# First expert layer in unsplit float32, with the split parts' buffers lent to weights and to gathered rows

## The chip, the cores and the metric

The kernel is one program on one core of one Trainium2 chip. The metric is device time in microseconds, from the program's start to its end; less is better. A profiled execution lists every instruction of the engines: TensorE (PE for matmuls, PEld for weight loads), VectorE (DVE), ScalarE (ACT), GpSimd (POOL), and SyncE (SP), which here only issues DMAs.

## The reference

Two blocks run one after the other, in float32, on 256 tokens of width 1024. The first (gated state-space, linear recurrence and retention branches, then a convolutional FFN) makes x. The second has two layers over x and a context xc of 256 tokens; each layer mixes tokens and then adds an expert layer (`peer_ffn`), in layer 0 to both streams, in layer 1 to x alone. The change concerns the expert layer of layer 0, for x.

```python
def peer_ffn(h, wq, sub_keys, eu, ev):            # eu, ev: 16384 experts x 1024
    def one(t):                                   # t: 128 tokens x 1024
        q = (t @ wq).reshape(TOKEN_BLOCK, PEER_HEADS, 2, PEER_DK // 2)
        s = jnp.einsum("thpd,hpnd->thpn", q, sub_keys)
        st, it = lax.top_k(s, PEER_TOPK)          # 16 of 128 keys, twice a head
        ...                                       # best 16 of the 256 pairs
        e = jnp.take_along_axis(cidx, pos, axis=-1)
        g = jax.nn.softmax(best, axis=-1)
        u = jnp.take(eu, e, axis=0)               # 8 heads x 16 = 128 experts a token
        act = jax.nn.gelu(jnp.einsum("thkd,td->thk", u, t), approximate=False)
        return jnp.einsum("thk,thkd->td", (g * act), jnp.take(ev, e, axis=0))
...
    h2 = rmsnorm_2(x, norm2_g) * (1.0 + sc2) + sh2
    x = x + g2 * peer_ffn(h2, peer_wq, peer_keys, peer_u, peer_v)
    if need_ctx:                                  # layer 0
        ...
        xc = xc + g2c * peer_ffn(h2c, peer_wq, peer_keys, peer_u, peer_v)
```

## The kernel before

Activations lie with 128 of the 1024 channels on the partitions, as tiles of [128, 8, 256 tokens]. A weight tile is [128, 1024] float32 (8 blocks of 128 x 128). Two ways of multiplying exist. In the split way (`mm3`, L295) a weight is loaded to a buffer `raw`, ScalarE rounds it to a high part `whi` of type float32r (L257), VectorE or GpSimd subtracts to a low part `wlo` (L258), and TensorE makes 24 matmuls: high x high and high x low alternating (L301, L302), then low x high (L304). In the whole way (`W(..., True)`) the raw weight is multiplied by float32 activations in 8 matmuls, each of which the profile shows as two instructions.

`Stream` (L260) is the weight stream. The instance `W` has a ring of three `raw` buffers, and rings of three `whi` and three `wlo`, 4 KB a partition each; every load is issued by SyncE (L271). `pattern` says which engine makes the low parts: in the expert layer of layer 0 it is GpSimd ("G").

The expert layer has two forms. For the context of layer 0 it is sparse (`Sparse`, L1496): `work` makes 512 steps, and each gathers one expert row a token for 128 tokens by an indirect DMA that GpSimd issues (L1529), into one of four `gr` buffers, three rows ahead of use. In the first 256 steps VectorE multiplies the row with the tokens and sums it into a dot product (L1540); in the others it adds the row, times its weight, to `gy` (L1546, L1548). The steps are laid beside other work: `steps(n)` moves `work` on by n rows, and the program text has 86 of them in the token mixer of x in layer 0 before the dense layer begins.

For x the form is dense (`peer`, L1583): all 16384 experts are computed for all 256 tokens, and a matrix A of gate weights, mostly zero, picks those that count. `norm_split` (L364) makes the normed input, in layer 0 as high part `Hh`, low part `Hl` and whole `H`. `queries` (L1487) makes the keys' queries, `choose2` the top 16s, and `spread` (L1446) scatters them into A in DRAM. Then:

- `first` (L1614) is one unit: the weight `pu` for 128 experts, matmuls with the input into a bank `pp`, and a GELU on ScalarE to `gt` (L1623). In layer 0 odd units are whole (L1619), even ones split (L1621). 13 groups of 8 units, 104, are made ahead (L1650 to L1665) while choosing and spreading go on, and each `gt` is stored to DRAM (`GX`, L1657).
- `ustage` (L1673) loads A for a group of 8 units (`At`, L1678) and each `gt` again (L1684), or makes it for the last three groups, and multiplies the two (L1688). `vstage` (L1697) multiplies by `pv`, eight weight tiles `d` a group, whole in layer 0 (L1703), and adds to x (L1704).

`tick(0)` after each unit made ahead is `steps(1.0)`, `tick(1)` after each `d` is `steps(2.6)`, and `tick(2)` runs what is left and adds the context's result (`far.end`). `kept` is how many of the 104 tiles stay in SBUF in place of `GX`; it is 0 in layer 0 and 51 in layer 1.

The order of instructions on each engine is laid down when the kernel is built, by a scheduler that takes the program text as priority and its own estimate of when things are ready; on the chip each engine keeps that order. An engine can so be ahead of the text with work that was ready early.

Of the kernel before, what the change touches and what calls it, by code (L numbers as in the profile page):

```python
# [18 lines left out]
P = 128  # L19
T = 256  # L20
# [167 lines left out]
def build(tc, I, out, off, dbg=None):  # L188
# [71 lines left out]
    class Stream:  # L260
# [6 lines left out]
            s.turn, s.pattern = 0, pattern  # L267

        def __call__(s, ap, whole=False):
            raw = s.raw.tile([P, 1024], F32, name="raw")  # L270
            nc.sync.dma_start(raw, ap)  # L271
            if whole:
                return raw.rearrange("p (k n) -> p k n", k=8)
            hi = s.hl.tile([P, 1024], F32R, name="whi")
            lo = s.hl.tile([P, 1024], F32R, name="wlo")
            e = G if s.pattern[s.turn % len(s.pattern)] == "G" else V
            s.turn += 1
            split(hi, lo, raw, e)
            return hi.rearrange("p (k n) -> p k n", k=8), lo.rearrange("p (k n) -> p k n", k=8)
# [15 lines left out]
    def mm3(ps, w, x, ks=range(8), x0=0, start=True, stop=True):  # L295

        wh, wl = w
        xh, xl = x
        ks = list(ks)
        for j, k in enumerate(ks):  # L300
            PE.matmul(ps, wh[:, k], xh[:, x0 + k], start=start and j == 0, stop=False)  # L301
            PE.matmul(ps, wh[:, k], xl[:, x0 + k], start=False, stop=False)  # L302
        for j, k in enumerate(ks):
            PE.matmul(ps, wl[:, k], xh[:, x0 + k], start=False, stop=stop and j == len(ks) - 1)  # L304
# [59 lines left out]
    def norm_split(rg, x, rstd, gcol, shcol, hi, lo, whole=None):  # L364

        for k in range(8):
            h = rg.t1()
            V.scalar_tensor_tensor(h, x[:, k], gcol(k), rstd, op0=ALU.mult, op1=ALU.mult)
            if whole is not None:
                A.activation(whole[:, k], h, AF.Identity, bias=shcol(k))  # L370
            if shcol is None:
                A.activation(hi[:, k], h, AF.Copy)
                V.tensor_sub(lo[:, k], h, hi[:, k].bitcast(F32))
            else:
                A.activation(hi[:, k], h, AF.Identity, bias=shcol(k))
                V.scalar_tensor_tensor(lo[:, k], h, shcol(k), hi[:, k].bitcast(F32),  # L376
                                       op0=ALU.add, op1=ALU.subtract)
# [1106 lines left out]
                    nc.sync.dma_start(Ad[t * 8 + tg], stg.rearrange("p g e n k -> p (g e n k)"))  # L1484
                yield

    def queries(l, w, bk, sp, h):  # L1487
        n = h[0].shape[-1]
        q = sp.tile([P, 8, n], F32, name="pq", bufs=1)
        for hd in range(8):  # L1490
            ps = bk.proj()[:, :n]
            mm3(ps, w(I["wq"][l, hd]), h)
            A.activation(q[:, hd], ps, AF.Copy)
        return q

    class Sparse:  # L1496
# [1 line left out]


        def __init__(m, l, s, pool):  # L1500
            m.l, m.s = l, s
            tile_ = lambda shape, dt, name: pool.tile(shape, dt, name=name, bufs=1)
            m.h = tile_([P, 2, 1024], F32, "gh")
            m.idx = tile_([P, 2, P], U32, "gi")
            m.wt = tile_([P, 2, P], F32, "gw")
            m.dot = tile_([P, 2, P], F32, "gd")
# [12 lines left out]
        def work(m, pool, nbuf):  # L1519

            m.y = pool.tile([P, 2, 1024], F32, name="gy", bufs=1)
            todo = [(w, t, k) for w in range(2) for t in range(2) for k in range(P)]
            got = []

            def gather():
                if len(got) < len(todo):
                    w, t, k = todo[len(got)]
                    r = pool.tile([P, 1024], F32, name="gr", bufs=nbuf)
                    G.indirect_dma_start(r, None, I[("us", "vs")[w]],  # L1529
                                         bass.IndirectOffsetOnAxis(ap=m.idx[:, t, k:k + 1], axis=0))  # L1530
                    got.append(r)

            for _ in range(nbuf - 1):
                gather()
            for n, (w, t, k) in enumerate(todo):
                gather()
                r = got[n]
                got[n] = None
                if w == 0:
                    V.scalar_tensor_tensor(r, r, 1.0, m.h[:, t], op0=ALU.mult, op1=ALU.mult,  # L1540
                                           accum_out=m.dot[:, t, k:k + 1])
                    if k == P - 1:
                        A.activation(m.dot[:, t], m.dot[:, t], AF.Gelu)
                        V.tensor_mul(m.wt[:, t], m.wt[:, t], m.dot[:, t])
                elif k == 0:
                    V.tensor_scalar(m.y[:, t], r, m.wt[:, t, k:k + 1], None, op0=ALU.mult)  # L1546
                else:
                    V.scalar_tensor_tensor(m.y[:, t], r, m.wt[:, t, k:k + 1], m.y[:, t], op0=ALU.mult, op1=ALU.add)  # L1548
                yield
# [33 lines left out]
    def peer(l, streams, ahead, nproj, kept=0, side_work=None, tick=lambda n: None, ends=None):  # L1583
# [5 lines left out]
        s, = streams  # L1589
        xs = ExitStack()  # L1590
        hp = xs.enter_context(TP(f"H{l}"))
        Hh = hp.tile([P, 8, N], F32R, name="Hh")
        Hl = hp.tile([P, 8, N], F32R, name="Hl")
        gp = xs.enter_context(TP(f"pg{l}", 4))
        Ads = [dram.tile([16, P, 2048], F32, name=f"A{l}{s}") for s in streams]
        H = hp.tile([P, 8, N], F32, name="H") if l == 0 else None
        GX = dram.tile([ahead * 8 - kept, P, N], F32, name=f"GX{l}")
        gk = xs.enter_context(TP(f"pk{l}", kept, side="right")) if kept else None
        mark(f"norm2{l}")
# [3 lines left out]
        with TP(f"n2{l}") as sm:  # L1603
            rg = Ring(sm, 8, 0)
            for j in range(ns):
                norm_split(rg, X[s], rstd_cm(rg, bk.misc, X[s], 8, D), sc_col(l, 1, s), sh_col(l, 1, s),
                           Hh[:, :, j * T:(j + 1) * T], Hl[:, :, j * T:(j + 1) * T], H)
        Y, At, GT = {}, {}, {}

        na = ahead * 8  # L1610
# [2 lines left out]

        def first(g, j, pool=gp):  # L1614
            ps = bk.proj()[:, :N]
            if H is not None and j % 2:
                w = W(I["pu"][l, g * 8 + j], True)
                for k in range(8):
                    PE.matmul(ps, w[:, k], H[:, k], start=k == 0, stop=k == 7)  # L1619
            else:  # L1620
                mm3(ps, W(I["pu"][l, g * 8 + j]), (Hh, Hl))  # L1621
            gt = pool.tile([P, N], F32, name="gt")
            A.activation(gt, ps, AF.Gelu)  # L1623
            return gt

        with ExitStack() as ls:
            sp, sm, so = [ls.enter_context(TP(f"{n}{l}", 2)) for n in ("rt", "rs", "rz")]
            j = 0
            W.pattern = "G"
            q = queries(l, W, bk, sp, [z[:, :, j * T:(j + 1) * T] for z in (Hh, Hl)])  # L1630
            sls = [sp.tile([P, 2, P, 2, 2], F16, name="sl") for t in range(2)]
            bo = Banks(ls, f"po{l}", 0, 2)

            def pieces():
                mark(f"choose{l}{s}")
                for _ in choose2(l, q, sls, sm, bks.proj, bk):
                    yield 0.85
                    mark(f"choose{l}{s}")
                for t in range(2):
                    mark(f"spread{l}{s}")  # L1640
                    for _ in spread(sls[t], Ads[j], t, so, bo.misc):
                        yield 1.42
                        mark(f"spread{l}{s}")

            if side_work:
                side_work(ls)

            run, credit = pieces(), 0.0
            W.pattern = "G" if l == 0 else "GV"
            for g in range(ahead):  # L1650
                for i in range(8):
                    mark(f"ahead{l}")
                    n = g * 8 + i
                    if n in stay:
                        GT[n] = first(g, i, gk)
                    else:
                        nc.sync.dma_start(GX[place[n]], first(g, i))  # L1657
                    tick(0)
                    credit += 1
                    while credit > 0 and run:  # L1660
                        w = next(run, None)
                        if w is None:
                            run = None
                            break
                        credit -= 1 / w  # L1665
            for _ in run or ():
                pass
# [103 lines left out]
    if stages >= 2:  # L1771
        with ExitStack() as fr:
# [25 lines left out]
            if stages >= 3:  # L1798
                ends = []

                def tick(n):
                    if n < 2:
                        steps((1.0, 2.6)[n])
                    else:
                        for _ in run:
                            pass
                        far.end(ends[0])

                peer(0, (0,), 13, 3, 0, side, tick, ends)
        gs.close()  # L1810
    if stages >= 4:
        with ExitStack() as fs:
# [54 lines left out]
```

## Time and profile before

| | |
|---|---|
| median of 3 runs | 3745.09 us (3743.55 to 3750.69) |
| profiled execution: time, span | 3736.46 us, 3734.7 us |
| busy share of the span: PE, DVE, POOL, ACT | 84%, 68%, 44%, 35% |
| mean granted clock of TensorE | 0.927 |
| read from HBM, written | 823.34 MB, 55.18 MB |

The span is the time from the first instruction to the last; the little around it is the difference to the execution's time. An engine's busy share is an average over stages with different limits, so it doesn't name the limit of any one stage. A row of a lines view gives, after the count, the busy time, the mean duration in ns, then the idle time of the engine just before such instructions and what ended it.

### The profile page before, as it was taken

The page shows a single profiled execution, that of the slowest core. Times are in us where ns is not written, and L with a number is a line of the kernel's source. Part 1 is how long each engine was busy: PE and PEld are TensorE (multiplying, and loading weights), DVE is VectorE, ACT ScalarE, POOL GpSimd, SP SyncE. Part 2 cuts the span into 40 slices and gives each one's busy share as a digit, 9 for nine tenths or more (in the row PEclk, how much of TensorE's full clock was granted, in tenths as well). Part 3 has the DMA queues.
Part 4 walks back from the last instruction along what each step waited for, and adds up shares of the span by engine and source line. Part 5 has one row for each costly group of instructions (what it writes and reads, how often), then busy time and mean ns, then how long its engine had stood idle before and what let it go on. Part 6 is the DMA issues. An engine that isn't in the chain of part 4 may idle for free. (4 is left out here: it accounts for less than half of the span.)

```text
span 3734.7 us, 57168 instructions
## 1 busy us (share of the span) xinstructions
PE 3153.2 (84%) x21589; PEld 2856.7 (76%) x21589; DVE 2547.0 (68%) x4819; ACT 1298.9 (35%) x2302; POOL 1646.6 (44%) x1141
## 2 busy tenths in 40 slices
PE   8899987899675587777767877999888999999998
PEld 6699976899563376666656666888776999999998
DVE  7845757578988778978866666422655788677755
ACT  4544446454244122222200000011463546544443
POOL 1233213155677677777744444121663544322222
PEclk9999998999797799989888888999999999999999
DMA  7665541355785889899999999754434667877754
GB/s 246 245 185 160 162 130 51 116 181 178 232 290 163 309 282 306 306 341 352 357 382 355 382 364 365 267 169 163 130 119 162 197 195 272 278 237 244 242 198 136
DMA packets 327397, 882.29 MB, mean 236 GB/s; under 512 B 29521, under 2 KB 142161, under 8 KB 316753
## 3 DMA queue, kind: packets, MB, share of 16 engines
q1 hardware_dynamic: 252528, 607.65, 49.1%
q0 software_dynamic: 73872, 269.52, 19.9%
q8 instruction: 170, 2.79, 0.3%
q10 hardware_dynamic: 720, 1.47, 0.1%
q14 instruction: 107, 0.87, 0.1%
HBM read 823.34 MB, written 55.18 MB: 235 GB/s over the span
## 5 line engine op out<-in xcount | busy, mean ns | idle before, releaser
L258 POOL TENSOR_TENSOR wlo<-raw,whi 128x1024 fp32r<-128x1024 f32 x325 | 808.5, 2490 | 1288.3 <-ACT whi L257 1131.1
L257 ACT ACTIVATE whi<-raw 128x1024 fp32r<-128x1024 f32 x644 | 680.3, 1058 | 1653.9 <-DMA raw<-pu 963.8
L1703 PE MATMUL pp<-gt,raw 128*128 128x256 f32 x2048 | 495.3, 405 | 109.9 <-DMA raw<-pv 48.1
L1703 PEld LDWEIGHTS pp<-gt,raw 128*128 128x128 f32 x2048 | 413.5, 204 | 190.8 <-DVE gt L1688 39.5
L258 DVE TENSOR_TENSOR wlo<-raw,whi 128x1024 fp32r<-128x1024 f32 x319 | 400.8, 1257 | 203.9 <-ACT whi L257 193.5
L1540 DVE SCALAR_TENSOR_TENSOR gr<-gr,gh 128x1024 f32<-128x1024 f32 x256 | 384.4, 1510 | 115.8 <-DMA gr<-us,gi 115.1
L1548 DVE SCALAR_TENSOR_TENSOR gy<-gr,gw,gy 128x1024 f32<-128x1024 f32 x254 | 345.8, 1361 | 171.3 <-DMA gr<-vs,gi 169.9
L301 PE MATMUL pp<-Hh,whi 128*128 128x256 f32 x1664 | 430.3, 296 | 23.2 <-ACT gt L1623 17.2
L1529 POOL DMA_INDIRECT gr<-vs,gi x256 | 297.1, 1160 | 309.6 <-DVE gy L1548 243.3
L302 PE MATMUL pp<-Hl,whi 128*128 128x256 f32 x1664 | 414.8, 287 | 0.0
L1529 POOL DMA_INDIRECT gr<-us,gi x256 | 331.3, 1294 | 177.4 <-DVE gr L1540 85.1
L301 PEld LDWEIGHTS pp<-Hh,whi 128*128 128x128 f32 x1664 | 323.7, 195 | 34.3 <-ACT gt L1623 23.6
L302 PEld LDWEIGHTS pp<-Hl,whi 128*128 128x128 f32 x1664 | 323.9, 195 | 3.5 <-DVE Hl L376 1.6
L304 PE MATMUL pp<-Hh,wlo 128*128 128x256 f32 x1664 | 243.3, 290 | 50.6 <-POOL wlo L258 41.9
L304 PEld LDWEIGHTS pp<-Hh,wlo 128*128 128x128 f32 x1664 | 220.1, 196 | 58.3 <-POOL wlo L258 48.7
L1711 PE MATMUL pp<-yh,whi 128*128 128x256 f32 x1024 | 251.5, 285 | 11.5 <-ACT yh L257 11.5
L1712 PE MATMUL pp<-yl,whi 128*128 128x256 f32 x1024 | 253.1, 286 | 9.4 <-DVE yl L258 9.3
L1619 PE MATMUL pp<-H,raw 128*128 128x256 f32 x1024 | 251.9, 403 | 4.2 <-ACT gt L1623 2.4
L1619 PEld LDWEIGHTS pp<-H,raw 128*128 128x128 f32 x1024 | 204.5, 204 | 33.8 <-ACT gt L1623 2.6
L1688 DVE TENSOR_TENSOR gt<-gt,At 128x256 f32<-128x256 f32 x256 | 143.2, 602 | 106.3 <-ACT gt L1623 57.8
L301 PE MATMUL pp<-pairh,whi 128*128 128x256 f32 x672 | 179.6, 302 | 33.4 <-ACT t L1078 11.2
L1711 PEld LDWEIGHTS pp<-yh,whi 128*128 128x128 f32 x1024 | 193.9, 192 | 14.4 <-ACT yh L257 14.0
(480 smaller groups left out, 6479.0 us busy)
## 6 DMA issues: line engine op xcount, KB each, us to landing
raw<-pu SPq DMA_DIRECT2D x256, 512.0 KB, 4.6
raw<-pv SPq DMA_DIRECT2D x256, 512.0 KB, 4.7
raw<-w SPq DMA_DIRECT2D x136, 512.0 KB, 3.8
aw<-ada SPq DMA_DIRECT2D x48, 1024.0 KB, 5.1
raw<-wf SPq DMA_DIRECT2D x72, 512.0 KB, 3.7
A<-stg SPq DMA_DIRECT2D x32, 1024.0 KB, 7.1
At<-A SPq DMA_DIRECT2D x32, 1024.0 KB, 8.0
GX<-gt SPq DMA_DIRECT2D x157, 128.0 KB, 5.1
```

The source lines that it names most:

```text
L257: A.activation(hi, src, AF.Copy)
L258: (eng or V).tensor_sub(lo, src, hi.bitcast(F32))
L301: PE.matmul(ps, wh[:, k], xh[:, x0 + k], start=start and j == 0, stop=False)
L302: PE.matmul(ps, wh[:, k], xl[:, x0 + k], start=False, stop=False)
L304: PE.matmul(ps, wl[:, k], xh[:, x0 + k], start=False, stop=stop and j == len(ks) - 1)
L1529: G.indirect_dma_start(r, None, I[("us", "vs")[w]], bass.IndirectOffsetOnAxis(ap=m.idx[:, t, k:k + 1], axis=0))
L1540: V.scalar_tensor_tensor(r, r, 1.0, m.h[:, t], op0=ALU.mult, op1=ALU.mult, accum_out=m.dot[:, t, k:k + 1])
L1548: V.scalar_tensor_tensor(m.y[:, t], r, m.wt[:, t, k:k + 1], m.y[:, t], op0=ALU.mult, op1=ALU.add)
L1619: PE.matmul(ps, w[:, k], H[:, k], start=k == 0, stop=k == 7)
L1703: PE.matmul(ps, w[:, j], Y[g, j], start=j == 0, stop=j == 7)
L1711: PE.matmul(ps, wh[:, j], yh, start=j == 0, stop=False)
L1712: PE.matmul(ps, wh[:, j], yl, start=False, stop=False)
```

## The change

In layer 0 the queries and all units of `first` take the whole way; `norm_split` makes only `H` there, and `Hh` and `Hl` aren't allocated. A whole load of `Stream` takes turns between a `raw` buffer and a `whi` buffer. During the dense layer 0 rows of `Sparse` are issued six ahead, and every second one goes to a `wlo` buffer of `W`. 18 of the 104 `gt` tiles stay in SBUF. The pace of rows is 1.2 for each unit ahead and 2.2 for each `d`, for 1.0 and 2.6.

```diff
--- before.py
+++ after.py
@@ -267,10 +267,14 @@
             s.turn, s.pattern = 0, pattern
 
         def __call__(s, ap, whole=False):
+            if whole:
+                s.turn += 1
+                raw = (s.raw.tile([P, 1024], F32, name="raw") if s.turn % 2
+                       else s.hl.tile([P, 1024], F32R, name="whi").bitcast(F32))
+                nc.sync.dma_start(raw, ap)
+                return raw.rearrange("p (k n) -> p k n", k=8)
             raw = s.raw.tile([P, 1024], F32, name="raw")
             nc.sync.dma_start(raw, ap)
-            if whole:
-                return raw.rearrange("p (k n) -> p k n", k=8)
             hi = s.hl.tile([P, 1024], F32R, name="whi")
             lo = s.hl.tile([P, 1024], F32R, name="wlo")
             e = G if s.pattern[s.turn % len(s.pattern)] == "G" else V
@@ -368,6 +372,7 @@
             V.scalar_tensor_tensor(h, x[:, k], gcol(k), rstd, op0=ALU.mult, op1=ALU.mult)
             if whole is not None:
                 A.activation(whole[:, k], h, AF.Identity, bias=shcol(k))
+                continue
             if shcol is None:
                 A.activation(hi[:, k], h, AF.Copy)
                 V.tensor_sub(lo[:, k], h, hi[:, k].bitcast(F32))
@@ -1484,12 +1489,17 @@
                     nc.sync.dma_start(Ad[t * 8 + tg], stg.rearrange("p g e n k -> p (g e n k)"))
                 yield
 
-    def queries(l, w, bk, sp, h):
-        n = h[0].shape[-1]
+    def queries(l, w, bk, sp, h, whole=None):
+        n = T
         q = sp.tile([P, 8, n], F32, name="pq", bufs=1)
         for hd in range(8):
             ps = bk.proj()[:, :n]
-            mm3(ps, w(I["wq"][l, hd]), h)
+            if whole is None:
+                mm3(ps, w(I["wq"][l, hd]), h)
+            else:
+                x = w(I["wq"][l, hd], True)
+                for k in range(8):
+                    PE.matmul(ps, x[:, k], whole[:, k], start=k == 0, stop=k == 7)
             A.activation(q[:, hd], ps, AF.Copy)
         return q
 
@@ -1498,7 +1508,7 @@
 
 
         def __init__(m, l, s, pool):
-            m.l, m.s = l, s
+            m.l, m.s, m.extra, m.ahead = l, s, None, 3
             tile_ = lambda shape, dt, name: pool.tile(shape, dt, name=name, bufs=1)
             m.h = tile_([P, 2, 1024], F32, "gh")
             m.idx = tile_([P, 2, P], U32, "gi")
@@ -1525,15 +1535,17 @@
             def gather():
                 if len(got) < len(todo):
                     w, t, k = todo[len(got)]
-                    r = pool.tile([P, 1024], F32, name="gr", bufs=nbuf)
+                    if m.extra and len(got) % 2:
+                        r = m.extra.tile([P, 1024], F32R, name="wlo").bitcast(F32)
+                    else:
+                        r = pool.tile([P, 1024], F32, name="gr", bufs=nbuf)
                     G.indirect_dma_start(r, None, I[("us", "vs")[w]],
                                          bass.IndirectOffsetOnAxis(ap=m.idx[:, t, k:k + 1], axis=0))
                     got.append(r)
 
-            for _ in range(nbuf - 1):
-                gather()
             for n, (w, t, k) in enumerate(todo):
-                gather()
+                while len(got) < min(len(todo), n + m.ahead + 1):
+                    gather()
                 r = got[n]
                 got[n] = None
                 if w == 0:
@@ -1589,11 +1601,15 @@
         s, = streams
         xs = ExitStack()
         hp = xs.enter_context(TP(f"H{l}"))
-        Hh = hp.tile([P, 8, N], F32R, name="Hh")
-        Hl = hp.tile([P, 8, N], F32R, name="Hl")
+
+        Hh, Hl, H = None, None, None
+        if l == 0:
+            H = hp.tile([P, 8, N], F32, name="H")
+        else:
+            Hh = hp.tile([P, 8, N], F32R, name="Hh")
+            Hl = hp.tile([P, 8, N], F32R, name="Hl")
         gp = xs.enter_context(TP(f"pg{l}", 4))
         Ads = [dram.tile([16, P, 2048], F32, name=f"A{l}{s}") for s in streams]
-        H = hp.tile([P, 8, N], F32, name="H") if l == 0 else None
         GX = dram.tile([ahead * 8 - kept, P, N], F32, name=f"GX{l}")
         gk = xs.enter_context(TP(f"pk{l}", kept, side="right")) if kept else None
         mark(f"norm2{l}")
@@ -1604,7 +1620,7 @@
             rg = Ring(sm, 8, 0)
             for j in range(ns):
                 norm_split(rg, X[s], rstd_cm(rg, bk.misc, X[s], 8, D), sc_col(l, 1, s), sh_col(l, 1, s),
-                           Hh[:, :, j * T:(j + 1) * T], Hl[:, :, j * T:(j + 1) * T], H)
+                           Hh, Hl, H)
         Y, At, GT = {}, {}, {}
 
         na = ahead * 8
@@ -1613,7 +1629,7 @@
 
         def first(g, j, pool=gp):
             ps = bk.proj()[:, :N]
-            if H is not None and j % 2:
+            if l == 0:
                 w = W(I["pu"][l, g * 8 + j], True)
                 for k in range(8):
                     PE.matmul(ps, w[:, k], H[:, k], start=k == 0, stop=k == 7)
@@ -1627,7 +1643,7 @@
             sp, sm, so = [ls.enter_context(TP(f"{n}{l}", 2)) for n in ("rt", "rs", "rz")]
             j = 0
             W.pattern = "G"
-            q = queries(l, W, bk, sp, [z[:, :, j * T:(j + 1) * T] for z in (Hh, Hl)])
+            q = queries(l, W, bk, sp, (Hh, Hl), H)
             sls = [sp.tile([P, 2, P, 2, 2], F16, name="sl") for t in range(2)]
             bo = Banks(ls, f"po{l}", 0, 2)
 
@@ -1798,15 +1814,17 @@
             if stages >= 3:
                 ends = []
 
+                far.extra, far.ahead = W.hl, 6
+
                 def tick(n):
                     if n < 2:
-                        steps((1.0, 2.6)[n])
+                        steps((1.2, 2.2)[n])
                     else:
                         for _ in run:
                             pass
                         far.end(ends[0])
 
-                peer(0, (0,), 13, 3, 0, side, tick, ends)
+                peer(0, (0,), 13, 3, 18, side, tick, ends)
         gs.close()
     if stages >= 4:
         with ExitStack() as fs:
```

## Rows read from the trace of the kernel before

**Rows 1.** Windows, whole core: length, busy time by engine, clock, DMA share, GB/s.

```profile
924.00:1341.00 417.00, 262.17 (x1604) 222.48 (x1603) 342.96 (x678) 144.96 (x299) 288.02 (x220) 0.81 0.73 247
1341.00:1906.00 565.00, 424.97 (x2613) 376.51 (x2612) 464.02 (x834) 132.63 (x247) 408.51 (x276) 0.89 0.94 333
1906.00:2367.00 461.00, 352.88 (x1394) 289.57 (x1395) 305.02 (x361) 1.06 (x2) 201.67 (x194) 0.86 1.00 368
2367.00:2590.00 223.00, 219.21 (x1139) 194.61 (x1137) 52.66 (x82) 24.74 (x44) 31.62 (x15) 1.00 0.54 176
```

**Rows 2.** Windows, L1540 alone (its instructions in brackets), first stretch.

```profile
924.00:1341.00 417.00, 182.65 (x259) 0.81 0.73 247
```

**Rows 3.** Windows, L1548 alone, second and third stretch.

```profile
1341.00:1906.00 565.00, 100.95 (x63) 0.89 0.94 333
1906.00:2367.00 461.00, 243.51 (x190) 0.86 1.00 368
```

**Rows 4.** Windows, L1704 alone, last two stretches.

```profile
1906.00:2367.00 461.00, 41.20 (x86) 0.86 1.00 368
2367.00:2590.00 223.00, 20.31 (x42) 1.00 0.54 176
```

**Rows 5.** Waits, 1341 to 1906: total us, times, longest.

```profile
ACT whi L257 <- DMA raw<-pu: 310.6, 49, 11.4
...
PE pm L1479 <- DVE ow L1459: 49.5, 19, 6.0
...
PE pp L304 <- POOL wlo L258: 38.4, 22, 5.3
```

**Rows 6.** Waits of SyncE's queue, 1341 to 1906.

```profile
SPq L1657 <- ACT gt L1623: 179.4, 44, 11.0
SPq L271 <- POOL wlo L258: 163.4, 46, 9.4
```

**Rows 7.** Lines, 1906 to 2367.

```profile
L1703 PE MATMUL pp<-gt,raw 128*128 128x256 f32 x1393 | 352.9, 417 | 108.4 <-DMA raw<-pv 46.7 <-DVE gt L1688 33.9 <-DVE xT L1704 25.0
...
L1529 POOL DMA_INDIRECT gr<-vs,gi x188 | 200.1, 1064 | 255.7 <-DVE gy L1548 209.9 <-DMA gr<-vs,gi 30.3 <-issue 14.1
...
L1688 DVE TENSOR_TENSOR gt<-gt,At 128x256 f32<-128x256 f32 x83 | 30.3, 416 | 4.6 <-DMA gt<-GX 4.2
```

**Rows 8.** Lines, 1341 to 1906 (one engine's view each).

```profile
L1540 DVE SCALAR_TENSOR_TENSOR gr<-gr,gh 128x1024 f32<-128x1024 f32 x127 | 206.2, 1632 | 59.7 <-DMA gr<-us,gi 59.5
...
L258 POOL TENSOR_TENSOR wlo<-raw,whi 128x1024 fp32r<-128x1024 f32 x51 | 125.1, 2453 | 8.6 <-ACT whi L257 7.9
...
L1479 PE MATMUL pm<-oo,ow 128*128 128x128 f16 x512 | 41.2, 233 | 52.5 <-DVE ow L1459 49.5 <-ACT stg L1481 2.1 <-ACT gt L1623 0.7
```

**Rows 9.** The page's DMA issues: count, KB each, median us to landing.

```profile
At<-A SPq DMA_DIRECT2D x32, 1024.0 KB, 8.0
GX<-gt SPq DMA_DIRECT2D x157, 128.0 KB, 5.1
```

**Rows 10.** Timeline of TensorE in the fourth stretch: start us, us.

```profile
2452.94 0.39 PE L301 MATMUL pp<-Hh,whi 128*128 128x256 f32 x1 [0.29 <-ACT gt L1623]
...
2456.19 3.61 PE L1619 MATMUL pp<-H,raw 128*128 128x256 f32 x16
2459.64 16.57 PE L1703 MATMUL pp<-gt,raw 128*128 128x256 f32 x76
```

**Rows 11.** Durations (ns min/median/max) and landing, of L1540, L1548, L1529.

```profile
L1540 DVE SCALAR_TENSOR_TENSOR gr<-gr,gh x256: 1189/1216/5377, 932.1 to 1716.3; 128x1024 f32<-128x1024 f32 x128
...
L1548 DVE SCALAR_TENSOR_TENSOR gy<-gr,gw,gy x254: 1270/1284/3972, 1722.0 to 2367.2; 128x1024 f32<-128x1024 f32 x127
...
DMA to landing us min/median/max: 4.1/7.0/11.6
```

**Rows 12.** Timeline of ScalarE in the norm: first and last of 16.

```profile
1306.65 0.51 ACT L370 ACTIVATE H<-t,mod 128x256 f32<-128x256 f32 x1 [13.33 <-DVE t L368]
...
1312.65 0.50 ACT L375 ACTIVATE Hh<-t,mod 128x256 fp32r<-128x256 f32 x1
```

## Prediction

> **What bounds the kernel now.** I read the windows of the whole core first, cut where the work around the change changes its kind [rows 1]. Four stretches follow one another: 924 to 1341 us (the rest of layer 0's mixer, with rows gathered beside it), 1341 to 1906 ("ahead": the 104 first units of the dense expert layer, one 512 KB weight each, beside choosing, spreading and rows), 1906 to 2367 (the second matmuls beside the last rows), and 2367 to 2590 (the same without rows). The reader is to see that the DMA share is 1.00 at 368 GB/s in the third stretch and 0.94 at 333 GB/s in the second, and only 0.54 in the fourth, where TensorE has its full clock and is busy for 219 of 223 us. So the third stretch is bound by DMA, the fourth by TensorE, and the second lies 10% under the rate that DMA holds next door.
>
> Then I counted the work in each. A row is 128 partitions x 1024 float32, 0.524 MB. A row of the first kind is two instructions on L1540 (the product and the read of its accumulator), so 259 of them are 130 rows by 1341 us [rows 2]. In the second stretch 127 follow [rows 8], then one on L1546 and 63 on L1548: 191. The third has 190 on L1548 [rows 3], which makes 511 of the 512; the last falls on its end. The second matmuls' results (L1704) number 86 in the third stretch and 42 in the fourth [rows 4]. So while rows run from 1341 on, 382 rows (512 less 130) pass beside 104 + 86 = 190 weight units: 2.01 rows a unit.
>
> Last, why the second stretch doesn't fill DMA: the waits. ScalarE's copy of the high part waits 310.6 us for the weight to land, and TensorE waits 38.4 us for the low part from GpSimd [rows 5]. SyncE's queue holds the next weight for 163.4 us until GpSimd has made a low part and so freed the raw buffer, and holds a store (L1657), with the loads behind it, 179.4 us for the GELU, which stands on ScalarE behind those copies [rows 6]. Three raw buffers, half of which pass through ScalarE and GpSimd, keep too few loads in flight. Rows are short of buffers as well: in the third stretch GpSimd idles 209.9 us until VectorE has used a row [rows 7].
>
> **The change part by part, at the same order of rows and units.** The sum is made against the profiled execution's 3736.46 us (span 3734.7); the median of the runs is 8.6 us above that, which I add at the end.
>
> *Second stretch.* All 52 split units become plain float32, so the 51 low parts on GpSimd (125.1 us) and the copies on ScalarE go [rows 8]. SyncE no longer waits for them; it has six weight buffers in place of three, and rows have seven in place of four, up to six in flight. I take it that DMA then fills as in the third stretch. The bytes are 565 us x 333 = 188 MB, less 18 stores of 128 KB that stay on chip [rows 9] (2.4 MB): 185.8 MB at 368 is 505 us, **-60**. What could hide under it is shorter. TensorE: a float32 unit takes 3.45 us, start to start, and a split one 3.25 [rows 10], so 104 x 3.45 = 359, with the spread's 41.2 [rows 8] 400. VectorE: 464 us busy [rows 1], less 73: its 127 rows on L1540 took 1632 ns beside GpSimd's work [rows 8] where the median of all is 1216, and the 63 on L1548 took 1602 (100.95 us over 63) [rows 3] against 1284 [rows 11]; some 390. Both lie under 505, so the float32 price of 52 x 0.2 = 10 us is covered; uncovered it is paid.
>
> On that rate the Trainium skill says something else: "DMA: Bandwidth & Descriptors", section Specifications, gives about 358 GB/s as the limit of HBM for one core. The third stretch held 368 [rows 1], so the measurement decides; by the page the 185.8 MB would take 519 us and this term would be -46.
>
> *Third stretch.* Of the 18 tiles kept, 86/104 are used here, 15 loads of 128 KB: 2.0 MB at 368, **-5**. More buffers give nothing else where DMA is full.
>
> *Fourth stretch.* 12 of its 24 first units were split: 12 x 0.2 = **+2**.
>
> *Before them.* The norm loses 8 of 16 activations on ScalarE at 0.4 us from start to start (16 between 1306.65 and 1312.65) [rows 12] and as many subtractions on VectorE beside them: -3. Eight queries in float32: 8 x 0.2 = +2. Together **-1**. By program order 86 rows are used and 90 issued before the expert layer starts, but the trace has 130 used by then [rows 2]; so in the new kernel rows from 90 on may take low-part buffers that the output projection's splits still want. At worst its 8 units wait one landing each, 7 us [rows 11]: +56; at best 20 rows move into a stretch whose DMA share is 0.73, 20 x 0.524/368, -28. I take 0 and keep both ends.
>
> That is -64. *Order.* The order on VectorE is fixed when the kernel is built, and it fixes how many rows pass per unit. One unit less by the end of the rows saves 0.524 MB of weight and some 0.26 MB of its other traffic (1/8 of 1 MB of gates and a 128 KB tile [rows 9]): 0.786/368, 2.14 us of the full DMA; and it adds 3.45 us on TensorE in the fourth stretch: **+1.31 us a unit**. The pace in the diff pulls both ways. From 1.0 to 1.2 steps a unit puts 21 rows more into the second stretch (+30 us); 2.6 to 2.2 thins those after: 170 rows at 2.21 x 2.2/2.6 = 1.87 a unit need 91 units of (0.786 + 1.87 x 0.524)/368 = 4.80 us, 437 for the 461 us; the fourth stretch loses 5 units. In all some -10: the low end. But 190 rows in the second stretch, where the pace alone asks for 104, say that rows go when buffers and VectorE allow, not by the pace. With 7 buffers for 4, rows per unit could reach 3.5: 109 units, 81 x 1.31 = +106, the high end. VectorE speaks against that: of a unit's 3.45 us it has 2.55 beside L1704 (41.20 us over 86) [rows 4] and L1688 (416 ns) [rows 7], room for 2.0 rows of 1284 ns [rows 11]. I take 2.14, nearest to before: 178.5 units, 11.5 x 1.31 = **+15**.
>
> Sum: -60 - 5 + 2 - 1 + 15 = -49; 3736.5 - 49 = 3687; with the 8.6 us, **3695** (1.3% faster).
>
> **The rivals.**
>
> *Rows crowd out weights (the other side).* The place is VectorE's order and the shared DMA; the deeper ring lets rows run ahead, units arrive late, and TensorE is left with a longer stretch alone at 3.45 us a unit. For it: GpSimd's 209.9 us of waiting for a row's buffer [rows 7]. Against it: VectorE's room. It eats the gain of 64 when 64/1.31 = 49 units are missing: 141 units, 2.7 rows each. At 3.0 rows (127 units) the time is 3745 - 64 + 63 x 1.31 = 3764; at 3.5 it is 3787.
>
> *Weights gain on rows.* With six weight buffers SyncE's queue always has loads waiting. If the two streams then share DMA half and half, a unit's 0.786 MB at 184 GB/s takes 4.27 us, in which 1.5 rows pass; 382 rows last for 255 units, nearly all, and TensorE has no stretch alone: 65 x 1.31 = 85 less, 3745 - 64 - 85 = 3596. For it: in the third stretch TensorE still waits for weights (46.7 us, a wait that deeper loads can fill) [rows 7]. Against: the order on VectorE stays what the build made it, 2.2 rows a unit. The Trainium skill, "DMA: Bandwidth & Descriptors", section Queues, rings and completion order, states such a sharing: each DMA engine goes round-robin over the queues that have work, packet by packet. By that rule this rival follows if both queues are always full; the third stretch, with three weight buffers, shows rows taking 1.16 MB for 0.786 MB a unit, so they are not shared evenly there.
>
> *The change doesn't fill DMA.* TensorE also waits 49.5 us in the second stretch for VectorE's spread [rows 5], and VectorE, strictly in order, waits for rows in front of it. If that is the holder, the stretch stays at 565 and only the costs remain: -5 + 2 - 1 + 15 = +11 (with the float32 price of 10 paid too, +21): 3756 to 3766.
>
> **How the numbers follow.** Forecast, rows at 1.9 to 2.4 a unit and DMA filled by half or more: 0.60, its own range 3660 to 3730. Rows crowd (2.5 and more): 0.16, of which 0.05 is still faster, 0.02 same, 0.09 slower. Weights gain (under 1.8): 0.12. No fill: 0.12, of which 0.03, 0.03, 0.06. A measurement of this kernel tells about 0.2% (7.5 us) from no change. A hundredth of the forecast's chance falls to the same side: faster 0.79, same 0.06, slower 0.15. The range leaves out the far half of the weights' gain and the worst of the crowding and of the low-part buffers: 3640 to 3757.
>
> **What the profile will show.** Right: no low parts on GpSimd between 1341 and the end of the layer; ScalarE's and SyncE's waits for them gone; "ahead" near 505 us (some 525 with more rows in it) at 360 GB/s or more; the last row between 2250 and 2310; 174 to 195 units done by then; rows on VectorE near 1220 ns. Wrong: "ahead" still near 333 GB/s with TensorE waiting for the spread (no fill); rows ending before 2200 with a TensorE-bound stretch over 300 us (crowding); rows lasting to the end of the layer (weights gain). Were the time outside what these stretches sum to, some stage that I left untouched has moved.

## The result and the profile after

The changed kernel takes 3661.48 us (median of 3 runs, 3660.28 to 3664.39) against 3745.09: a ratio of 0.9775 [0.9753, 0.9797], 2.2% faster. The forecast was 3695, with 3640 to 3757 around it. The profiled execution took 3660.28 us (span 3658.5), 76.2 less than that of before.

Windows of the whole core, after, cut at the same events as [rows 1]: first unit, 104th unit, last row, last result of the second matmuls (columns as there).

```profile
924.00:1353.00 429.00, 266.37 (x1548) 233.59 (x1547) 352.68 (x705) 136.59 (x289) 278.99 (x223) 0.79 0.73 249
1353.00:1873.00 520.00, 433.57 (x2240) 365.39 (x2239) 425.19 (x853) 91.29 (x196) 325.71 (x263) 0.91 1.01 396
1873.00:2208.00 335.00, 252.81 (x1033) 210.37 (x1032) 234.37 (x280) 0.38 (x1) 157.55 (x144) 0.88 1.04 388
2208.00:2515.00 307.00, 304.05 (x1402) 267.22 (x1402) 56.77 (x127) 15.04 (x34) 6.05 (x7) 0.99 0.56 181
```

Read down the first number: 417, 565, 461, 223 before, now 429, 520, 335, 307. The stretches beside rows lose 171 us, and the stretch in which TensorE is alone, busy for 304 of 307 us, gains 84. Read down the last: 333 and 368 GB/s have become 396 and 388, both above the rate that the forecast took as DMA's own.

The rows on VectorE in the second and third stretch (L1540 is now L1552, two instructions a row; L1548 is now L1560), windows of each line alone:

```profile
1353.00:1873.00 520.00, 143.18 (x236) 0.91 1.01 396
...
1353.00:1873.00 520.00, 137.35 (x107) 0.91 1.01 396
1873.00:2208.00 335.00, 187.11 (x146) 0.88 1.04 388
```

That is 118 + 107 rows and the first of the second kind (one instruction on L1558), 226 in the second stretch (191 before), and 147 in the third, again with one on L1558. The results of the second matmuls (L1720, was L1704) by the last row:

```profile
1873.00:2208.00 335.00, 30.16 (x63) 0.88 1.04 388
2208.00:2515.00 307.00, 31.43 (x65) 0.99 0.56 181
```

So 104 + 63 = 167 units are done when the rows end, not 190 [rows 4]: 2.2 rows a unit, not 2.0.

Lines of the second stretch, after, shapes apart:

```profile
L1552 DVE SCALAR_TENSOR_TENSOR wlo<-wlo,gh 128x1024 f32<-128x1024 f32 x64 | 78.5, 1226 | 38.4 <-DMA wlo<-us,gi 38.2
...
L1552 DVE SCALAR_TENSOR_TENSOR gr<-gr,gh 128x1024 f32<-128x1024 f32 x54 | 65.9, 1220 | 3.6 <-DMA gr<-us,gi 3.6
...
L1639 ACT ACTIVATE gt<-pp 128x256 f32<-128x256 f32 x103 | 39.0, 383 | 334.3 <-PE pp L1635 269.5 <-issue 49.3 <-DMA GX<-gt 8.7
```

Half of the rows lie in buffers called wlo, the lent low parts. A row costs VectorE 1226 or 1220 ns where it took 1632 beside GpSimd's splits [rows 8]. ScalarE's idle time now ends with TensorE, and little waits for it: over the whole stretch TensorE stands 15.3 us for such a GELU. SyncE's queue in the same stretch:

```profile
SPq L274 <- PE pp L1635: 219.4, 60, 18.6
SPq L1673 <- ACT gt L1639: 85.9, 19, 18.6
```

Its wait for GpSimd's low part (163.4 us) [rows 6] is gone. Its store still waits for the GELU, 85.9 us where it was 179.4 [rows 6]. Most of all it now waits for TensorE to free one of six weight buffers: weights are ahead of their user.

### The profile page after: what moved, and what is told of

Read it like the earlier page. It is cut to its first block, busy times and chain, and to the rows that moved or that the text cites. A ratio compares the mean times of both kernels' runs of the same rounds, so it can differ in the third digit from the quotient of the medians.

```text
span 3658.5 us, 55605 instructions
## 1 busy us (share of the span) xinstructions
PE 3149.5 (86%) x21013; PEld 2849.3 (78%) x21013; DVE 2451.1 (67%) x4811; ACT 1234.4 (34%) x2222; POOL 1477.2 (40%) x1069
## 5 line engine op out<-in xcount | busy, mean ns | idle before, releaser
L258 POOL TENSOR_TENSOR wlo<-raw,whi 128x1024 fp32r<-128x1024 f32 x253 | 629.8, 2492 | 1236.4 <-ACT whi L257 1071.9
L1719 PE MATMUL pp<-gt,raw 128*128 128x256 f32 x1024 | 251.8, 400 | 70.8 <-DVE gt L1704 66.8
L1719 PEld LDWEIGHTS pp<-gt,raw 128*128 128x128 f32 x1024 | 204.0, 201 | 106.5 <-DVE gt L1704 58.4
L305 PE MATMUL pp<-Hh,whi 128*128 128x256 f32 x1088 | 272.9, 289 | 1.2 <-ACT Hh L380 1.2
L1635 PE MATMUL pp<-H,whi 128*128 128x256 f32 x1024 | 248.1, 397 | 28.3 <-ACT gt L1639 15.3
L1704 DVE TENSOR_TENSOR gt<-gt,At 128x256 f32<-128x256 f32 x256 | 133.2, 552 | 203.3 <-DMA At<-A 91.8
L1552 DVE SCALAR_TENSOR_TENSOR gr<-gr,gh 128x1024 f32<-128x1024 f32 x172 | 228.0, 1330 | 42.0 <-DMA gr<-us,gi 41.8
L1542 POOL DMA_INDIRECT wlo<-vs,gi x128 | 173.7, 1357 | 202.3 <-DVE gy L1560 183.0
L1719 PE MATMUL pp<-gt,whi 128*128 128x256 f32 x1024 | 241.4, 390 | 13.9 <-DVE xT L1720 13.8
L1635 PEld LDWEIGHTS pp<-H,whi 128*128 128x128 f32 x1024 | 202.3, 200 | 62.5 <-ACT gt L1639 16.1
L1719 PEld LDWEIGHTS pp<-gt,whi 128*128 128x128 f32 x1024 | 200.3, 197 | 47.6 <-DVE xT L1720 18.3
```

Of the source, the lines that this page charges most:

```text
L258: (eng or V).tensor_sub(lo, src, hi.bitcast(F32))
L1542: G.indirect_dma_start(r, None, I[("us", "vs")[w]], bass.IndirectOffsetOnAxis(ap=m.idx[:, t, k:k + 1], axis=0))
L1704: V.tensor_mul(gv, gv, At[g][:, :, :, j])
L1719: PE.matmul(ps, w[:, j], Y[g, j], start=j == 0, stop=j == 7)
```

## The experiments

Each ran beside the kernel before on its chip; ratios are to that. Where two runs stood beside different executions of the kernel before, the difference of their ratios, times 3745 us, is the fairer figure.

**The change in parts.** Three runs take the two lent rings out, one at a time and both: the first edit here is that of the rows, the second that of the weights.

```diff
-                far.extra, far.ahead = W.hl, 6
...
-                raw = (s.raw.tile([P, 1024], F32, name="raw") if s.turn % 2
-                       else s.hl.tile([P, 1024], F32R, name="whi").bitcast(F32))
+                raw = s.raw.tile([P, 1024], F32, name="raw")
```

Rows with 4 buffers, 3 ahead:

> The change without the rows' part: rows keep four buffers and go three ahead; weights keep six buffers, float32 and 18 kept tiles stay. Theory A (the weights' ring and the end of the splits carry the gain; with fewer row buffers rows pass slower per unit, 2.0 in place of 2.2, and DMA stays at 380 GB/s or more in the units made ahead): 3640 to 3675 us, no slower than the change, the TensorE-bound stretch after the last row shorter than its 306 us. Theory B (the rows' deeper ring carries it, since it is what lifts DMA over 368 GB/s): DMA falls back to 340 to 370 GB/s there and the time is 3695 or more.

Weights with 3 buffers:

> The change without the weights' part: whole loads take the three raw buffers only; rows keep seven buffers. Theory A: weights starve beside rows, more rows pass per unit (2.5 or more by the last row), the stretch without rows grows, 3700 us or more. Theory B: 3655 to 3680, as the change.

Both, which leaves the plain float32, the 18 kept tiles and the new pace:

> Float32 and the 18 kept tiles alone, with three weight buffers and four row buffers as before. Theory C (the splits were the trouble: GpSimd's work that slows VectorE and the waits for low parts; the rings add little): 3690 us or less. Theories A and B (the rings carry it): 3710 to 3745, DMA in the units made ahead at 350 GB/s or less.

Measured: 3719.79 us (0.9915 [0.9884, 0.9947]), 3680.82 (0.9811 [0.9776, 0.9845]) and 3728.62 (0.9947 [0.9926, 0.9968]). Second and third stretch of each, windows of the whole core; rows with 4 buffers:

```profile
1337.00:1898.00 561.00, 441.95 (x2241) 372.09 (x2239) 420.82 (x848) 90.79 (x196) 294.78 (x252) 0.88 0.97 363
1898.00:2291.00 393.00, 279.82 (x1134) 230.77 (x1134) 250.34 (x302) 0.38 (x1) 172.25 (x157) 0.87 0.98 355
```

Weights with 3 buffers:

```profile
1345.00:1894.00 549.00, 445.19 (x2242) 366.02 (x2243) 436.85 (x870) 91.51 (x199) 330.35 (x267) 0.92 1.01 393
1894.00:2226.00 332.00, 262.42 (x1032) 211.54 (x1030) 226.56 (x265) 0.21 (x1) 163.32 (x141) 0.88 1.00 367
```

Neither ring lent:

```profile
1335.00:1913.00 578.00, 443.06 (x2240) 367.71 (x2239) 431.80 (x865) 90.76 (x196) 300.81 (x261) 0.90 0.97 364
1913.00:2271.00 358.00, 271.99 (x1092) 224.36 (x1093) 238.84 (x287) 0.23 (x1) 158.23 (x146) 0.87 1.00 364
```

The rows' ring is the largest part: by the ratios it takes off 51 us without the weights' ring and 52 with it. In the second stretch it takes DMA from 364 to 393 and from 363 to 396 GB/s. The weights' ring gives some 13 us on top of it, and there the third stretch goes from 367 to 388; alone it gives 12 us. Both of these are small: the intervals of the two runs compared overlap each time. So theory B is borne out by the first two runs (the second lies 1 us over its bound) and A is not. In the third the time fell where A and B had it, but the second stretch's 364 GB/s did not (350 or less).

Float32, kept tiles and pace give 20 us together; float32 alone was not run. The second stretch goes at 364 GB/s where it was 333, with GpSimd's splits gone; pace and kept tiles leave that rate as it is (396 in both runs below), so it is put down to the splits. That stretch is none the shorter for it, 578 us for 565, since 120 + 105 + 1 = 226 rows pass in it for 191; the third is, 358 for 461. In the runs with 4 row buffers 172 units are done by the last row, in those with 7 it is 167: most of the shift from 190 comes without either ring.

**Pace and kept tiles**, one edit a run.

```diff
-                        steps((1.2, 2.2)[n])
+                        steps((1.0, 2.6)[n])
...
-                peer(0, (0,), 13, 3, 18, side, tick, ends)
+                peer(0, (0,), 13, 3, 0, side, tick, ends)
```

> The change with the pace of rows of before (1.0 and 2.6). If rows go when buffers and VectorE allow and the pace in the text hardly binds, the time is within 10 us of the change's 3661 and rows per unit stay at 2.2 by the last row. If the pace sets the order, there are some 21 rows fewer before the second matmuls and more beside them, and the time moves by 10 us or more.

> The change with no first units' tile kept on chip: 18 more stores and 18 more loads of 128 KB. If both stretches are bound by DMA, the 4.7 MB cost 12 us at 390 GB/s: 3668 to 3678 us. If these transfers are hidden, the time is within 5 us of the change's 3661.

The old pace: 3660.70 us (0.9759 [0.9728, 0.979]), 167 units by the last row: the pace doesn't bind. No tile kept: 3671.98 (0.9788 [0.9763, 0.9813]). That is 11 us more by the medians and 5 by the ratios, inside the intervals, so time alone doesn't tell the two forecasts apart. 18 stores and 18 loads of 128 KB are 4.7 MB, 12 us at 396 GB/s; that the second stretch takes 533 us against 520 at the same 396 GB/s speaks for their being paid.

**A GELU among the rows.** Near the first unit ScalarE waits 18.4 us for row 128, the last of the first half of the tokens, to apply the GELU to their dot products (`gd`), and TensorE waits 8.8 us for ScalarE. The first unit's own GELU (`gt`) stands right behind it (timeline of ScalarE, after; the queries' copies in between left out):

```profile
1352.08 0.31 ACT L1555 ACTIVATE gd<-gd 128x128 f32<-128x128 f32 x1 [18.45 <-DVE wlo L1552]
...
1352.82 0.39 ACT L1639 ACTIVATE gt<-pp 128x256 f32<-128x256 f32 x1
```

One run asks for the GELU of the dot products 33 rows later in the text.

```diff
-                    if k == P - 1:
-                        A.activation(m.dot[:, t], m.dot[:, t], AF.Gelu)
+                    for u in ([0] if (t, k) == (1, 32) else [1] if (t, k) == (1, P - 1) else []):
+                        A.activation(m.dot[:, u], m.dot[:, u], AF.Gelu)
```

> The change with the GELU of the first half's dot products (ScalarE) asked for 33 rows later in the text, so that it doesn't fall on the start of the dense layer. If that GELU, waiting on VectorE's row 128, holds ScalarE's queue and so the queries' copies and TensorE (8.8 us before the second unit), the time falls by 6 to 12 us: 3649 to 3656. If VectorE's rows would hold the start anyway, it stays at 3661 within 4.

3662.02 us (0.9762 [0.9738, 0.9785]): no change. But the edit did not move what it was to move. The build put the GELU in the same place on ScalarE, and the wait is there as before:

```profile
1347.02 0.31 ACT L1555 ACTIVATE gd<-gd 128x128 f32<-128x128 f32 x1 [18.36 <-DVE wlo L1552]
```

TensorE's 8.8 us are there too. So this run doesn't tell whether that wait costs anything.

**How many buffers.** Rows 4 ahead in place of 6 with the same seven buffers (the first edit); then, with the second edit too, only one row in five in a lent buffer, so that a buffer comes free five rows later.

```diff
-                far.extra, far.ahead = W.hl, 6
+                far.extra, far.ahead = W.hl, 4
...
-                    if m.extra and len(got) % 2:
+                    if m.extra and len(got) % 5 == 4:
```

> The changed kernel with rows fetched 4 ahead in place of 6 (before: 3). If DMA's rate goes with the loads in flight, the first stretch of the expert layer runs between the 363 GB/s of 3 ahead and the 396 of 6, near 375, and the time is about 3697 us. If one more than before is enough, it stays at 396 and 3661; if only the deepest ring helps, 3715.

> The changed kernel with one row in five, not every second, in a lent low-part buffer, and rows fetched 4 ahead: a row's buffer now comes free five rows later, not four (as with the ring of 4) and not seven. The run with 4 ahead and seven buffers did not differ from 6 ahead, so buffers, not the order in the program, set how many rows are in flight. Landing theory: a row lands 7.0 us after its issue, so 3 in flight pass at most 0.43 rows a us, about what the first stretch of the expert layer now uses (225 in 520 us), and 4 in flight pass 0.57; then one buffer more gives nearly all of what seven give: 390 GB/s or more there and 3661 to 3672 us. Rival, each load in flight adds its share of the 33 GB/s between rings of 4 and 7: 374 GB/s, about 3700 us.

Four ahead: 3659.45 us (0.9772 [0.9729, 0.9816]), as with six: how far ahead the text asks doesn't bind, the number of buffers does. One in five: 3679.76 us (0.9803 [0.9771, 0.9835]), with these windows:

```profile
1338.00:1861.00 523.00, 431.61 (x2244) 362.84 (x2242) 422.73 (x847) 91.54 (x197) 300.27 (x254) 0.92 1.00 391
1861.00:2224.00 363.00, 258.22 (x1034) 213.40 (x1035) 239.30 (x289) 0.00 (x0) 174.29 (x150) 0.86 1.00 366
```

The landing theory is right on the second stretch, and neither is right on the time, which lies between theirs. In the second stretch one buffer more than before gives 391 of the 396 GB/s, as the landing theory says: at the 7.0 us a landing of before [rows 11], 3 in flight bound the rows at 0.43 a us; with 4 buffers they went at 220 in 561 us, 0.39, and with one more at 222 in 523, 0.42. In the third stretch the rate stays at 366, where seven buffers give 388. Why that stretch wants more was not settled.

**The order of rows and units.** The 307 us in which TensorE is alone are where the order costs. Two runs hold each row's fetch back until its unit's result is there: ScalarE copies the row's index with a bias of zero times that result. More rows go into the mixer ahead of the layer (10, 5, 10 steps for 6, 4, 6), and the second run has 1.8 and 1.45 steps a unit for the first's 1.5 and 1.7.

```diff
+                    ix = pool.tile([P, 1], U32, name="ix", bufs=8)
+                    A.activation(ix, m.idx[:, t, k:k + 1], AF.Identity, bias=m.gate)
...
+            A.activation(m.gate, ap, AF.Identity, scale=0.0)
...
-                        steps((1.2, 2.2)[n])
+                        steps((1.5, 1.7)[n])
```

> The change with rows held to the text's pace: the index of each row comes out of a ScalarE copy that waits for the unit (or the d) after which the text asks for the row; 130 rows are asked for in the mixer in place of 86, then 1.5 a unit and 1.7 a d. Theory A (the order of rows among units sets how long TensorE works without rows at the end, 1.4 us a unit): 200 units or more are done by the last row in place of 167, the stretch without rows is 200 us or less, and the time is 3585 to 3630. Rival (what is won there is lost by rows that now wait for units, DMA under 370 GB/s): 3650 or more.

> As g1 with 1.8 rows a unit and 1.45 a d: more rows in the units made ahead, where spread and choosing hold TensorE anyway. Theory A: within 15 us of g1, since the sum of rows and units is the same; the rival as in g1.

3774.48 us (1.0062 [1.0042, 1.0082]) and 3768.24 (1.0056 [1.003, 1.0081]): 0.6% slower than before, a miss for theory A. No stretch of TensorE alone is left, but the rest of the layer takes 753 us at 300 GB/s. Window of the whole core and, from 1950 to 2300 us, the longest waits, first of these two runs:

```profile
1845.00:2598.00 753.00, 583.37 (x2434) 487.76 (x2433) 378.92 (x478) 93.74 (x380) 240.00 (x226) 0.90 0.85 300
```

```profile
ACT z L1569 <- DVE xT L1729: 305.3, 66, 9.4
POOL wlo L1546 <- ACT ix L1545: 105.6, 35, 6.5
POOL gr L1546 <- ACT ix L1545: 101.3, 28, 7.4
DVE gy L1564 <- DMA gr<-vs,ix: 73.9, 44, 4.0
DVE gy L1564 <- DMA wlo<-vs,ix: 70.8, 46, 4.4
```

This is a ring: GpSimd waits for the index, the index for the unit's result on VectorE, VectorE for a row fetched too late, and the next unit stands behind that row. Rows that are fetched only when their unit is done can't use the deeper buffers.

So two further runs tie the order only: the rows are queued on VectorE behind the unit's result, while buffers still fetch ahead. The pace is 2.1 rows for each first unit, and 1.65 behind each second unit, 1.95 in the second run.

```diff
-                    V.scalar_tensor_tensor(X[s][:, d], ps, gate_col(l, 1, s, d), X[s][:, d], op0=ALU.mult, op1=ALU.add)
-                    tick(1)
+                    tick(1, V.scalar_tensor_tensor(X[s][:, d], ps, gate_col(l, 1, s, d), X[s][:, d],
+                                                   op0=ALU.mult, op1=ALU.add))
...
-                    if n < 2:
-                        steps((1.2, 2.2)[n])
+                    if n == 0:
+                        steps(2.1)
+                    elif n == 1:
+                        with tc.issue_after(getattr(v, "ins", v)):
+                            steps(1.65)
```

> The rows of the last two stretches are queued on VectorE behind the results of the second matmuls (2.1 steps for each first unit, 1.65 for each second unit), as an order only: no data is waited for, and the buffers still fetch rows ahead. By the build's order 304 rows are done when the first second unit's result is formed and all 512 only with the last of 128. Order theory: the TensorE-bound stretch of 307 us at the end is what is left of the gain; with rows beside all units it goes, 65 units at 1.43 us each, -93: about 3570 us; the whole of what DMA moves from 1353 us on (520 x 396 + 335 x 388 + 307 x 181, 392 MB) would take 1004 us at 390 GB/s in place of 1162, which bounds the gain at 158: not under 3503. Rival, VectorE in order: rows and units wait for each other as when the rows were held by data (3774), DMA falls under 330 GB/s in the third stretch, and the time is 3661 or more.

> As before, with 1.95 rows behind each second unit: by the build's order 304 rows at the first result, 512 at the 107th. Order theory: 44 of the 65 second units that stood alone now stand beside rows, 44 x 1.43 = -63: about 3598 us, with some 21 units (100 us) alone at the end. Rival, VectorE in order: 3661 or more, but nearer to the changed kernel than the run with 1.65.

3577.82 us (0.9541 [0.9499, 0.9583]) and 3622.48 (0.9651 [0.961, 0.9693]): both beat the changed kernel, the first by 2.3 points. Its windows:

```profile
1343.00:1835.00 492.00, 426.90 (x2242) 361.41 (x2243) 357.29 (x804) 91.21 (x199) 238.02 (x207) 0.93 0.96 367
1835.00:2424.00 589.00, 544.61 (x2410) 468.64 (x2409) 358.11 (x451) 13.58 (x33) 264.22 (x205) 0.97 0.97 357
2424.00:2429.00 5.00, 5.00 (x26) 4.32 (x24) 1.84 (x3) 1.02 (x2) 2.81 (x1) 1.00 0.07 26
```

The stretch of TensorE alone has shrunk from 307 us to 5. The row that matters is the second: TensorE is busy for 545 of 589 us, with rows beside it all the way, and DMA moves 357 GB/s, under the 388 of the changed kernel, so that TensorE is now the nearer limit. From the changed kernel's ratio, 0.0234 x 3745 = 88 us over 65 units is 1.35 us a unit; the milder run gives 0.0124 x 3745 = 46 over 44, 1.06. The forecast's price was 1.31. The first run came within 8 us of the order theory's 3570, the milder one 24 over its 3598; the rival's 3661 or more is out.

## Why the prediction was right, and where its sizes were not

The reasons held, the sum came out 34 us too high against the medians (27 against the profiled executions). That it came so near is in part luck: the terms left out 60 us of gain and 31 us of cost. Term by term, at the same order of rows and units:

| term | forecast | worked out with the measured rates and counts |
|---|---|---|
| second stretch | -60 | 185.8 MB at 396 GB/s = 469: -96 |
| third | -5 | 461 x 368 less 2.0 MB, 167.6 MB at 388 = 432: -29 |
| fourth | +2 | 304.05 us over 1402 instructions, 16 a unit: 3.47 us for 3.45; +2 kept |
| before them | -1 | first unit at 1353 for 1341: +12 |
| order | +15 | 23 units x (3.45 - 0.786/0.388 = 1.42): +33 |
| sum | -49 | -78; the spans say -76.2 |

**Second stretch: right mechanism, wrong ceiling.** The split was the holder: GpSimd's low parts and the waits behind them are gone, and DMA fills, so "the change doesn't fill DMA" is out. The step that failed is "I take it that DMA then fills as in the third stretch". With neither ring lent it did, at 364 GB/s. But the forecast read a share of 1.00 at 368 as a full DMA, and gave the deeper rings no rate above it; with seven row buffers for four the second stretch moved 396. The trace of before held the warning. Its view of DMA, third stretch in 40 slices of 11.5 us:

```profile
GB/s 395 386 389 368 346 322 358 379 353 362 361 390 346 412 398 382 378 339 371 369 404 371 378 366 309 370 385 384 347 392 369 352 385 391 375 270 384 380 388 323
```

The slices run from 270 to 412 GB/s: had 368 been a ceiling, no slice could have passed it by 12%.

**Third stretch: a step that failed outright.** "More buffers give nothing else where DMA is full" left out 24 us (-29 for -5). The parts run one ring at a time show it: 364 GB/s with neither, 355 with the weights' alone, 367 with the rows' alone, 388 with both. Here it takes both rings, and why was not settled.

**Before them: bounds right, value not.** Rows in lent buffers do disturb the end of the mixer: the first unit comes at 1335 and 1337 us in the two runs with none lent, and between 1343 and 1353 in the eight with every second row lent whose fetches were not held. The shift, +12 us here, lies inside the forecast's -28 to +56. GpSimd waits there for VectorE to give back a lent buffer. What the forecast had not in view is ScalarE: in all eight the GELU behind row 128 (counted from 0 it is 127, odd, and so in a lent buffer) stands waiting for it, 9.9 to 20.0 us, and the first unit's result comes 0.7 us behind that GELU. Without lent buffers the same wait is 5.8 and 5.4 us and ends 18 to 20 us before the first unit. So that GELU is the likely carrier of the delay; no run took it away, so this is not shown.

**Order: right price, wrong count.** The forecast chose 178.5 units, and it was 167; its window for the last row, 2250 to 2310, was missed (2208), and its mark for crowding, an end before 2200 with over 300 us alone, was nearly met (307). The choice of 2.14 rows a unit, "nearest to before", failed in the second stretch, and not by the lent rings: without either, 226 rows pass there too (191 before). Which of the parts left moved them was not tested; one that changed is VectorE's time for a row, 1220 ns for 1632. The argument that the pace does not bind held: 167 units with either pace. Crowding was real, at 2.2 rows and not 2.5: by the price above it took 33 us of a gain of over 110.

**Weights gain on rows** did not come. Both queues' packet times in the third stretch, after (queue 0 rows, queue 1 SyncE's loads and stores; packets, MB, share of 16 engines):

```profile
q0 software_dynamic: 20840, 75.85, 57.9%
q1 hardware_dynamic: 38704, 53.95, 45.5%
```

Rows still take 1.4 times what SyncE's queue moves. That queue is not always full: its longest wait in the same 335 us is for TensorE to free a weight buffer.

```profile
SPq L274 <- PE pp L1719: 148.0, 49, 7.7
```

The rule that the forecast set beside this rival, the round-robin of the Trainium skill, "DMA: Bandwidth & Descriptors", section Queues, rings and completion order, speaks of queues that have work; in no run here did SyncE's queue always have some, so its shares were not put to the test. The rival's gain itself, rows beside all units, is there to be had, and the order tied by hand got it (3577.82 us; the rival said 3596).

## What to carry to other kernels

A DMA share of 1.00 says that some transfer is always under way, not that no more fits (here 1.00 stood beside 364 to 391 GB/s): before taking a rate as the ceiling, look at its best slices, and count the loads in flight against the time one needs to land. A ring lent for free is worth trying even where DMA looks full. And when two streams share an engine in order, tie their order where the build leaves it to readiness, but not the fetch: against the changed kernel the same idea cost 2.9 points of the time before one way and gave 2.3 the other.

## What the hardware showed that was not expected

The share of DMA passes one: 1.04 at 388 GB/s, and the two queues' packet times above add to 103.4% of the engines' span. On some engine, then, packets overlap in time and the share counts that time twice; whether they are of one queue or of both is not shown.

One core alone moved 396 GB/s over 520 us; its fullest slices of the page read 414. The Trainium skill, "DMA: Bandwidth & Descriptors", section Bandwidth, gives 425 GB/s for a 16 MB load with the pair's other core idle, and about 358 where both cores stream. This kernel runs on one core, and the trace lies between the two, nearer the first; the forecast weighed only the second figure, as the limit of one core.
